# A two-layer attention and state-space trunk: states through the outputs' ring and one step ahead, last projections by token halves, zero products first, the last columns in parts

## The chip, the cores and the metric

The kernel runs on one core of a Trainium2 chip. The metric is the device time of one execution in microseconds (us), the median of several runs: less is better. TensorE is called PE, VectorE DVE or Vector, ScalarE ACT, GpSimd POOL; SyncE (SP) issues nearly all DMAs. Line numbers (L113) are those of the kernel before; in the changed kernel the same lines stand some two to thirty lines further down.

## The reference

A decoder trunk of two layers on 1024 tokens of width 1024, in float32. Each layer is x + RMSNorm(mixer(RMSNorm(x))).

```python
# layer 0: attention over three dilations (1, 4, 16), each a causal window of 129 keys, 16 heads of 64
proj = h @ w_in                       # queries, keys, values of 3 groups, and a gate z
o_g, lse_g = windowed_attention(q_g, k_g, v_g, rel_bias)
o = sum(softmax(lse)[g] * o_g)        # over the three groups
mixer = (o * silu(z)) @ w_out
# layer 1: a state-space layer, 64 groups of 16 channels, 64 complex states each
u, z = split(h @ w_in)
states = scan(a_bar, b_bar @ u)       # s[t] = a_bar * s[t-1] + bu[t]
y = Re(C @ states) + d * u
g = gelu(y)
y = g * sigmoid(g @ w_glu + b_glu)
mixer = (y * silu(z)) @ w_out
```

## The kernel before

Every large product is made of three matmuls: both operands are split into a rounded part and a rest (hi and lo: whi and wlo, hh and hl), and hi·hi, hi·lo and lo·hi are added in PSUM. One split is a cast on ACT and a subtraction on DVE or POOL (L86, L87). A projection of 128 output columns for 512 tokens (a token half, `th`) is 24 matmuls of 128x512 (`proj_half`). The order of instructions on every engine is fixed when the kernel is built, by a scheduler that follows the written order, the priorities (`high_priority`) and its own estimate of the times; each engine then works its list in order and waits where an input is missing.

**Start.** Eight tiles of 128 tokens are loaded. The gain of the norm, one row, is spread over all partitions by matmuls with a row of ones (tile `pg`, L747, copied by ACT at L748). Tile by tile (`norm_transpose0`) ACT sums the squares (L138), DVE finishes the norm (`rstd`, L73 to L78) and scales the tile by norm and gain in two halves (L143), PE transposes each half (`pst`, L130), ACT and DVE split it (hh, hl). The first values are projected at once (`psv`, L235 to L237) from weights `wvr`, which ACT casts and POOL subtracts.

**Layer 1.** The tiles of the attention's output are normed and transposed (`norm_transpose1`); the result is h1, four tiles of SBUF (hi and lo of two token halves) in the pool `pb`, whose slots are called b0 to b5. `in_order` then runs 16 projections, each for token half 0 and then 1, 32 steps of 24 matmuls (`psj`); the first eight give u, the last eight the gate z. The first two begin by halves of 256 columns, while the last tiles are still being transposed.

**The scan.** Between these steps stand the stages of eight channel groups e. Group e has its base at step t = (11e+2)/4 and each stage a distance d from it: loads, `ssm_input` (U, 5), `ssm_taps` (6), `ssm_states` (7), `ssm_outputs` (10). `ssm_states` multiplies BT and U (`pv`), turns and scans on DVE and POOL (T, L1381 to L1392) and leaves X (L1389 to L1393) in two tiles of half a group; `ssm_outputs` adds taps·U and CA·X (`py`, L1407 and L1408), puts the gelu together on ACT, POOL and DVE (Y) and stores it to DRAM (`y_dr`).

**GLU.** y is loaded again by token halves (`gy`, 16 loads of 128x512, L1476) into slots of a small ring and split into g0 and g1 (hi and lo, `pb`). The projections with w_glu start with a block: two weights, two token halves, products 0 to 6 of all four and then product 7 (`psb`, 96 matmuls). g0's lo part lies in b3, which the taps of groups 4 to 7 occupied; g1 lies in b4 and b5, which held h1's first half.

**Output.** `out_tiles` computes eight tiles of 128 tokens in two halves of 512 columns (`pso`); the last tile (`out_norm_last`) is normed at once and stored.

The pool `outs` (tag O, 4 buffers of 128x1024) serves the attention's outputs, z112 and the weights of the post norms (`post`).

Of the kernel before, what the change touches and what calls it, by code (L numbers as in the profile page):

```python
# [23 lines left out]
P = 128  # L24
# [9 lines left out]
EARLY = 4  # L34

# [679 lines left out]
def attention(c, a):  # L715
# [8 lines left out]
    with tc.tile_pool(name="vphase", bufs=1, side="right", reuse_waits="tile") as pool:  # L724
# [42 lines left out]
def in_order(c, srcs, h, use, after=None, start=None, ws=()):  # L767
# [109 lines left out]
def out_part(c, ps, g, w, i, n, ks):  # L877

    nc = c.nc
    gh, gl = g[i // 4]  # L880
    wh, wl = w[n]
    ts = slice(i % 4 * P, i % 4 * P + P)
    for n, k in ks:
        nc.tensor.matmul(ps, gh[:, k, ts], wh[:, k, :], start=n == 0, stop=False)  # L884
        nc.tensor.matmul(ps, gh[:, k, ts], wl[:, k, :], start=False, stop=False)  # L885
        nc.tensor.matmul(ps, gl[:, k, ts], wh[:, k, :], start=False, stop=n == KT - 1)  # L886
# [29 lines left out]
def out_norm_last(c, pss, post, x, done):  # L916

    nc = c.nc
    ss = c.small.tile([P, 2], F32, tag="ss2", name="ss2")
    ys = [c.slot("y") for _ in range(2)]  # L920
    sq = [c.slot("sq") for _ in range(2)]
    for n in range(2):
        nc.scalar.activation(sq[n], pss[n], AF.Square, accum_out=ss[:, n:n + 1])
        nc.vector.tensor_tensor(ys[n], pss[n], post[:, n * H:n * H + H], op=ALU.mult)
    r = rstd(c, ss)
    for n in range(2):
        ns = slice(n * H, n * H + H)
        nc.vector.scalar_tensor_tensor(x[:, ns], ys[n], r[:, 0:1], x[:, ns], op0=ALU.mult, op1=ALU.add)
        done(ns)


def out_tiles(c, g, w, post, res, done, order, late, last=None):
# [7 lines left out]
    for i in range(8):  # L940
# [4 lines left out]
        elif i < 7:  # L945
            for n in range(2):
# [3 lines left out]
        if i == 7 and last:  # L950
            out_norm_last(c, pss[i], post, x, lambda ns: last(x, ns))
# [416 lines left out]
def ssm_states(self):  # L1368
# [5 lines left out]
    self.X = []  # L1374
    for b in range(2):
        gs = slice(b * 4, b * 4 + 4)
        T1, T2, X = (c.ssm.tile([P, 4, P], F32, name=n, tag=n, bufs=2) for n in ("T1", "T2", "X"))
# [16 lines left out]
        self.X.append(X)  # L1394
# [28 lines left out]
def layer1(c, a, h1, ws):  # L1423
# [38 lines left out]
    for t in range(32, 39):  # L1462
        run(t)


def glu(c, a):
# [5 lines left out]
    for th, tags in enumerate((("b1", "b3"), ("b4", "b5"))):  # L1472
# [191 lines left out]
```

## Time and profile before

| | us |
|---|---|
| median of 3 runs (1678.32 to 1683.48) | 1678.59 |
| the profiled execution | 1679.3 |
| its span, first to last instruction | 1677.5 |
| PE busy | 1650.1 |
| DVE busy | 1011.9 |
| ACT busy | 712.2 |
| POOL busy | 460.0 |

The span is 1.8 us shorter than the profiled execution's time, and that execution is 0.7 above the median. A row of a timeline gives start, length, engine, line, operation, output and inputs, shape and count, and in brackets how long the engine was idle before it and what ended the idle time. A row of the waits gives engine, tile and line, what it waited for, the sum in us, how often, and the longest. A row of a group gives, after the bar, busy us and mean ns, then idle us before it and what ended most of it. A row of a stretch gives its length, then the busy us of PE, weight loads, DVE and ACT with their counts, the granted clock of PE, the DMA engines' share and GB/s.

### The profile page before, as it was taken

Reading aid. Unit: us, or ns where it says so; the run is one execution under the profiler, and the core shown is the slowest. Engines: PE = TensorE matmul, PEld = TensorE weight load, DVE = VectorE, ACT = ScalarE, POOL = GpSimd, SP = SyncE. Lnnn points to the kernel's source line nnn. Section 1 sums busy time; section 2 is a strip of 40 time slices with the busy share of each in tenths; the row PEclk is TensorE's granted clock in tenths of the full one; section 3 lists DMA queues with packets and bytes.
Section 4 is the critical chain, followed back from the end, with each engine's and each line's share of the span. In section 5 each row is a group of like instructions: output and inputs, shape, how many; then the busy total and the mean of one; then the engine's idle time right before and its main releaser. Section 6 shows DMA issues by size and latency. Waiting matters only on the chain.

```text
span 1677.5 us, 26337 instructions
## 1 busy us (share of the span) xinstructions
PE 1650.1 (98%) x9714; PEld 1390.6 (83%) x9714; DVE 1011.9 (60%) x2509; ACT 712.2 (42%) x1730; POOL 460.0 (27%) x303
## 2 busy tenths in 40 slices
PE   8999999999999999999999999999999999999998
PEld 6889999978888888888888888887788887867886
DVE  8698898625554554545455455557562888845533
ACT  5232223236455464645546464654452223343411
POOL 2000000131241514324161441404220344513121
PEclk9999999999999999999999999999999999989999
DMA  6213455531232414233252423318346979365432
GB/s 238 86 49 109 144 181 158 170 109 55 79 99 82 119 54 114 68 90 95 67 139 65 120 79 87 109 34 234 103 162 175 273 222 259 101 207 171 144 120 86
DMA packets 176857, 212.19 MB, mean 126 GB/s; under 512 B 37443, under 2 KB 133462, under 8 KB 176728
## 3 DMA queue, kind: packets, MB, share of 16 engines
q1 hardware_dynamic: 176728, 210.52, 42.3%
q8 instruction: 76, 1.25, 0.3%
q14 instruction: 53, 0.43, 0.1%
HBM read 153.51 MB, written 56.96 MB: 125 GB/s over the span
## 4 chain that ended last, share of the span: by engine, by line
PE 87%; DVE 7%; DMA 3%; issue 1%; POOL 1%; ACT 1%; SPq 0%; DVEq 0%; ACTq 0%; POOLq 0%
PE psj L113 46%; PE psq L376 11%; PE psl L474 5%; PE pso L551 4%; PE pt L502 4%; PE pso L886 3%; PE pso L885 3%; PE pso L884 3%; PE pso L577 1%; PE psb L113 1%; DVE T L1387 1%; PE psv L237 1%; DVE T L1392 1%; PE psv L236 1%; PE psv L235 1%
## 5 line engine op out<-in xcount | busy, mean ns | idle before, releaser
L113 PE MATMUL psj<-hh,wlo 128*128 128x512 f32 x896 | 358.2, 400 | 0.0
L113 PE MATMUL psj<-hh,whi 128*128 128x512 f32 x896 | 358.1, 400 | 0.0
L113 PE MATMUL psj<-hl,whi 128*128 128x512 f32 x896 | 355.2, 396 | 0.0
L87 POOL TENSOR_TENSOR wlo<-wraw,whi 128x1024 fp32r<-128x1024 f32 x48 | 115.2, 2399 | 395.9 <-ACT whi L86 380.8
L113 PEld LDWEIGHTS psj<-hh,whi 128*128 128x128 f32 x896 | 168.8, 188 | 37.0
L113 PEld LDWEIGHTS psj<-hh,wlo 128*128 128x128 f32 x896 | 168.8, 188 | 36.4
L113 PEld LDWEIGHTS psj<-hl,whi 128*128 128x128 f32 x896 | 168.7, 188 | 36.3
L491 ACT ACTIVATE lg<-lg,nm 128x128 f32<-128x128 f32 (+1 forms) x384 | 168.2, 442 | 37.3 <-DVE nm L486 37.3
L480 DVE CUSTOM_DVE_ANT_0 lg<-psl,T 128x128 f32<-128x128 f32 (+1 forms) x384 | 110.5, 347 | 88.7 <-PE psl L474 88.7
L86 ACT CAST whi<-wraw 128x1024 fp32r<-128x1024 f32 x80 | 83.7, 1046 | 163.8 <-PE psj L113 117.5
L376 PE MATMUL psq<-whi,v 128*128 128x256 f32 x640 | 120.3, 284 | 0.0
L87 DVE TENSOR_TENSOR ph<-pt,ph 128x512 fp32r<-128x512 f32 (+2 forms) x160 | 96.7, 622 | 15.3 <-ACT ph L86 13.1
L113 PE MATMUL psj<-h1h,whi 128*128 128x512 f32 (+1 forms) x272 | 105.0, 387 | 0.9 <-ACT h1h L86 0.9
L87 DVE TENSOR_TENSOR kl<-psj,kh 128x512 fp32r<-128x512 f32 x48 | 33.2, 692 | 120.1 <-ACT kh L86 119.5
L113 PE MATMUL psj<-h1l,whi 128*128 128x512 f32 (+1 forms) x272 | 104.1, 383 | 0.2 <-DVE h1l L87 0.2
L113 PE MATMUL psj<-h1h,wlo 128*128 128x512 f32 (+1 forms) x272 | 104.1, 383 | 0.0
L86 ACT CAST ph<-pt 128x512 fp32r<-128x512 f32 (+2 forms) x160 | 81.6, 530 | 46.5 <-PE pt L502 45.5
L376 PEld LDWEIGHTS psq<-whi,v 128*128 128x128 f32 x640 | 100.0, 189 | 1.2 <-issue 1.2
L376 PE MATMUL psq<-wlo,v 128*128 128x256 f32 x320 | 91.2, 286 | 0.7 <-DVE wlo L87 0.7
L551 PE MATMUL pso<-ph,vs 128*128 128x256 f32 (+1 forms) x544 | 86.6, 284 | 0.0
L502 PE MATMUL pt<-identr,lg 128*128 128x128 f32 x560 | 82.2, 276 | 0.0
L1253 POOL TENSOR_TENSOR Ks<-Ks,O 128x16 f32<-128x16 f32 x8 | 3.7, 462 | 284.0 <-ACT Ks L1251 284.0
(284 smaller groups left out, 3688.6 us busy)
## 6 DMA issues: line engine op xcount, KB each, us to landing
wraw<-in_w_in_dram SPq DMA_DIRECT2D x56, 512.0 KB
mw<-wt_dr SPq DMA_DIRECT2D x48, 256.0 KB
v<-in_w_v_dram SPq DMA_DIRECT2D x20, 512.0 KB
vp<-v_dr SPq DMA_DIRECT2D x16, 512.0 KB
wraw<-in_ssm_w_in_dram SPq DMA_DIRECT2D x16, 512.0 KB
v_dr<-v SPq DMA_DIRECT2D x30, 256.0 KB
rot_dr<-rt SPq DMA_DIRECT2D x48, 128.0 KB
ca_dr<-ca SPq DMA_DIRECT2D x32, 144.0 KB
```

The costliest lines, as they stand in the source:

```text
L86: c.last_hi = nc.scalar.copy(hi, src).ins
L87: return (engine or nc.vector).tensor_tensor(lo, src, f32(hi), op=ALU.subtract)
L113: nc.tensor.matmul(ps, a[:, s], b[:, k, :], start=first and k == 0 and n == 0, stop=k == KT - 1 and n == 2, skip_group_check=True)
L376: nc.tensor.matmul(o, r[x][:, k, ts], w[y][:, k, :], skip_group_check=True, start=i in (0, 4, 5) and t % 2 == k == n == 0, stop=k == 3 and ...
L474: nc.tensor.matmul(psl[:, h, o], x[HEADS[h], qs], y[HEADS[h], ks], start=j == js[0] and n == 0, stop=n == 2, skip_group_check=True)
L480: nc.vector.tensor_tensor_reduce(lg[:, h, j, 0:w], psl[:, h, o], bt[:, h, 256 - w:256], scale=1.0, scalar=-3.0e38, op0=ALU.add, op1=ALU.ma ...
L491: nc.scalar.activation(lg[:, h, j, 0:w], lg[:, h, j, 0:w], AF.Exp, bias=nm[:, h, b:b + 1], accum_out=ms[:, col:col + 1])
L502: c.nc.tensor.transpose(pt[:, n * P:(n + 1) * P], lg[:, h, j, part * P:part * P + P], c.ident)
L551: nc.tensor.matmul(o, l, r, start=n == 0, stop=n == len(jobs) - 1, skip_group_check=True)
L884: nc.tensor.matmul(ps, gh[:, k, ts], wh[:, k, :], start=n == 0, stop=False)
L885: nc.tensor.matmul(ps, gh[:, k, ts], wl[:, k, :], start=False, stop=False)
L886: nc.tensor.matmul(ps, gl[:, k, ts], wh[:, k, :], start=False, stop=n == KT - 1)
```

## The change

- **Zero products.** Eight matmuls of zeros (128x512, `idle`) stand first on PE; DVE writes the zeros first.
- **X in the ring O.** X of one group is one tile of the pool `outs`, with both halves, so that up to four groups can be alive. `ssm_input` stands at distance 4 and `ssm_states` at 6 for all groups but the first.
- **Last two projections by halves.** z's last two outputs (e = 14 and 15) are computed for token half 0 of both, then for half 1 of both.
- **GLU's inputs.** `gy` goes through three tiles of ring O, six half tiles, and may be issued only after the load of the last group's U. g0 lies in b1 and b4, g1 in b5 and b3.
- **Last columns in parts.** The second half of tile 7 is computed in two parts of 256 columns, each with its square and product by the post norm.

```diff
+IDLE = 8
@@ attention
+        zeros, idle = c.slot("zeros", F32R, tag="a"), c.psl.tile([P, H], F32, tag="psl", name="idle")
+        nc.vector.memset(f32(zeros), 0.0)
+        for n in range(IDLE):
+            nc.tensor.matmul(idle, zeros[:, 0:P], zeros, start=True, stop=True)
         nc.vector.memset(ones, 1.0)
@@ in_order
-    c.wide = 1 if start == "half" else c.wide
-    for e in range(len(ws), len(srcs)):
+    c.wide = int(start == "half")
+    pairs = 2 if start == "half" else 0
+    for e in range(len(ws), len(srcs) - pairs):
         w = load_w(c, srcs[e])
         for th in range(2):
             one(e, th, proj_half(c, w, h[th]))
+    ws = [(e, load_w(c, srcs[e])) for e in range(len(srcs) - pairs, len(srcs))]
+    for th in range(2):
+        for e, w in ws:
+            one(e, th, proj_half(c, w, h[th]))
@@ out_norm_last
+    ss = c.small.tile([P, 4], F32, tag="ss3", name="ss3")
+    ys = []
+    for n, (ps, cols) in enumerate(parts):
+        w = cols.stop - cols.start
+        y, sq = c.slot("y")[:, 0:w], c.slot("sq")[:, 0:w]
+        nc.scalar.activation(sq, ps, AF.Square, accum_out=ss[:, n:n + 1])
+        nc.vector.tensor_tensor(y, ps, post[:, cols], op=ALU.mult)
+        ys.append(y)
+        if n == 1:
+            nc.vector.tensor_tensor(ss[:, 3:4], ss[:, 0:1], ss[:, 1:2], op=ALU.add)
+    r = rstd(c, ss[:, 2:4])
+    for y, (ps, cols) in zip(ys, parts):
+        nc.vector.scalar_tensor_tensor(x[:, cols], y, r[:, 0:1], x[:, cols], op0=ALU.mult, op1=ALU.add)
@@ out_tiles
+            parts = [(pss[i][0], slice(0, H))]
+            for n in range(2):
+                cols = slice(n * 256, n * 256 + 256)
+                ps = c.psl.tile([P, H], F32, tag="psl", name="pso")[:, 0:256]
+                out_part(c, ps, g, w, i, 1, ks, cols)
+                parts.append((ps, slice(H + cols.start, H + cols.stop)))
@@ ssm_states
-        T1, T2, X = (c.ssm.tile([P, 4, P], F32, name=n, tag=n, bufs=2) for n in ("T1", "T2", "X"))
+    X2 = c.outs.tile([P, D], F32, tag="O", name="X", bufs=4).rearrange("p (b g n) -> p b g n", b=2, g=4)
+    self.X = [X2[:, b] for b in range(2)]
@@ layer1
-        for stage, d in ((ssm_loads, (-1, 2)[e] if e < 2 else 3), (ssm_input, 5), (ssm_taps, 6), (ssm_states, 7), (ssm_outputs, 10)):
+        for stage, d in ((ssm_loads, (-1, 2)[e] if e < 2 else 3), (ssm_input, 4 + (e == 0)), (ssm_taps, 6),
+                         (ssm_states, 6 + (e == 0)), (ssm_outputs, 10)):
@@ glu
-    for th, tags in enumerate((("b1", "b3"), ("b4", "b5"))):
+    ring = [x[:, n * H:n * H + H] for x in (c.outs.tile([P, D], F32, tag="O", name="gy", bufs=4) for _ in range(3)) for n in range(2)]
+    for th, tags in enumerate((("b1", "b4"), ("b5", "b3"))):
         for et in range(8):
-            y = c.slot("gy")
-            nc.sync.dma_start(y.rearrange("p (i n) -> p i n", i=4), y_view(c, et, th))
+            y = ring[(8 * th + et) % 6]
+            with tc.issue_after(last_input):
+                nc.sync.dma_start(y.rearrange("p (i n) -> p i n", i=4), y_view(c, et, th))
```

ACT's first instructions, before (ACTIVATE at L138 is a tile's sum of squares, `wvr` are the first value weights, `pg` the gain):

```order
L138 ACTIVATE v_117,ss<-v_118 128x1024
L748 COPY v_117<-pg 128x512
L86 CAST v_140<-wvr 128x1024 x2
L748 COPY v_117<-pg 128x512
L138 ACTIVATE v_117,ss<-v_118 128x1024
```

and of the change:

```order
L140 ACTIVATE v_117,ss<-v_118 128x1024
L88 CAST v_151<-wvr 128x1024
L755 COPY v_117<-pg 128x512
L88 CAST v_151<-wvr 128x1024
L140 ACTIVATE v_117,ss<-v_118 128x1024
L755 COPY v_117<-pg 128x512
```

The first cast of value weights has moved ahead of the first copy of the gain, and tile 1's sum of squares ahead of the second.

SP's list around the end of the scan, before (z_dr are stores of the gate, y_dr stores of y, gy the GLU's inputs; the two pairs of y_dr stores are those of groups 6 and 7):

```order
L1415 DMA y_dr<-Y_14745 128x512
L1415 DMA y_dr<-Y_14763 128x512
L1439 DMA z_dr<-z_14812 128x512
L98 DMA wraw<-in_w_glu_dram 128x1024
L1439 DMA z_dr<-z_14841 128x512
L1415 DMA y_dr<-Y_14845 128x512
L1415 DMA y_dr<-Y_14863 128x512
L1476 DMA gy<-y_dr 128x4x128 x3
L1439 DMA z_dr<-z_14912 128x512
L1476 DMA gy<-y_dr 128x4x128 x6
```

and of the change, from the first gy loads to the stores of group 7:

```order
L1506 DMA gy<-y_dr 128x4x128 x4
L1465 DMA z_dr<-z_14715 128x512
...
L1506 DMA gy<-y_dr 128x4x128 x2
L1441 DMA y_dr<-Y_14748 128x512
L1441 DMA y_dr<-Y_14766 128x512
L1465 DMA z_dr<-z_14821 128x512
L1506 DMA gy<-y_dr 128x4x128 x4
L984 DMA post<-in_ssm_post_norm_dram 128x1024
L1506 DMA gy<-y_dr 128x4x128
...
L1506 DMA gy<-y_dr 128x4x128 x2
L1441 DMA y_dr<-Y_14854 128x512
```

All gy loads stood behind the stores of group 7; now six stand ahead of those of group 6, and the load of the post norm's weights has come among them.

PE's last transposes for layer 1, before (`xn` is the normed tile):

```order
L113 MATMUL psj<-h1l_12779,whi 128x256
L130 MATMUL pst<-identr,xn 128x128 x4
L113 MATMUL psj<-h1h_12778,wlo 128x256
L130 MATMUL pst<-identr,xn 128x128 x4
L113 MATMUL psj<-h1h_12778,whi 128x256 x2
```

and of the change:

```order
L115 MATMUL psj<-h1l_12790,whi 128x256
L132 MATMUL pst<-identr,xn 128x128 x4
L115 MATMUL psj<-h1h_12789,wlo 128x256
L132 MATMUL pst<-identr,xn 128x128 x4
L115 MATMUL psj<-h1h_12789,whi 128x256
L115 MATMUL psj<-h1l_12790,whi 128x256
```

In the row "x2" the second of the two is the first product of the next 256 columns, which needs the tile just transposed; in the change nine more products of the first columns stand between. On PE the products pv and py of a group have 24 matmuls more between them for every group but the first. The last projections read, before: group 7's pv, 24 matmuls, group 6's py, 48, group 7's py, 48, psb; of the change: group 7's pv, 48, group 6's py, 48, group 7's py, 48, psb.

More of the change, by code (lines that the diff above doesn't have):

```diff
@@ L874, in attn_gate, with out_part @@
     return g, raw
-def out_part(c, ps, g, w, i, n, ks):
+def out_part(c, ps, g, w, i, n, ks, cols=slice(0, H)):
     nc = c.nc
@@ L883, in out_part @@
     for n, k in ks:
-        nc.tensor.matmul(ps, gh[:, k, ts], wh[:, k, :], start=n == 0, stop=False)
-        nc.tensor.matmul(ps, gh[:, k, ts], wl[:, k, :], start=False, stop=False)
-        nc.tensor.matmul(ps, gl[:, k, ts], wh[:, k, :], start=False, stop=n == KT - 1)
+        nc.tensor.matmul(ps, gh[:, k, ts], wh[:, k, cols], start=n == 0, stop=False)
+        nc.tensor.matmul(ps, gh[:, k, ts], wl[:, k, cols], start=False, stop=False)
+        nc.tensor.matmul(ps, gl[:, k, ts], wh[:, k, cols], start=False, stop=n == KT - 1)
 def out_bank(c, i):
@@ L913, in out_norm, with out_norm_last @@
         nc.gpsimd.tensor_tensor(x[:, ns], x[:, ns], y, op=ALU.add)
-def out_norm_last(c, pss, post, x, done):
+def out_norm_last(c, parts, post, x, done):
     nc = c.nc
-    ss = c.small.tile([P, 2], F32, tag="ss2", name="ss2")
-    ys = [c.slot("y") for _ in range(2)]
-    sq = [c.slot("sq") for _ in range(2)]
-    for n in range(2):
[L923 to L929, printed above, removed]
+    ss = c.small.tile([P, 4], F32, tag="ss3", name="ss3")
[11 more added lines that the diff above has]
+        nc.vector.scalar_tensor_tensor(x[:, cols], y, r[:, 0:1], x[:, cols], op0=ALU.mult, op1=ALU.add)
+    for n in range(2):
+        done(slice(n * H, n * H + H))
 def out_tiles(c, g, w, post, res, done, order, late, last=None):
@@ L945, in out_tiles @@
         elif i < 7:
-            for n in range(2):
+            for n in range(2 if i < 6 or not last else 1):
                 pss[i + 1][n] = out_half(c, g, w, i + 1, n, ks)
@@ L950, in out_tiles @@
         if i == 7 and last:
-            out_norm_last(c, pss[i], post, x, lambda ns: last(x, ns))
+            parts = [(pss[i][0], slice(0, H))]
[4 more added lines that the diff above has]
+                parts.append((ps, slice(H + cols.start, H + cols.stop)))
+            out_norm_last(c, parts, post, x, lambda ns: last(x, ns))
         else:
@@ L1373, in ssm_states @@
     lo, hi = slice(0, 64), slice(64, 128)
-    self.X = []
+    X2 = c.outs.tile([P, D], F32, tag="O", name="X", bufs=4).rearrange("p (b g n) -> p b g n", b=2, g=4)
+    self.X = [X2[:, b] for b in range(2)]
     for b in range(2):
         gs = slice(b * 4, b * 4 + 4)
-        T1, T2, X = (c.ssm.tile([P, 4, P], F32, name=n, tag=n, bufs=2) for n in ("T1", "T2", "X"))
+        T1, T2 = (c.ssm.tile([P, 4, P], F32, name=n, tag=n, bufs=2) for n in ("T1", "T2"))
+        X = self.X[b]
         pv = c.psl.tile([P, 4, P], F32, tag="psl", name="pv")
@@ L1393, in ssm_states @@
         nc.vector.tensor_tensor(X[:, :, 1:P], X[:, :, 1:P], T2[:, :, 0:P - 1], op=ALU.subtract)
-        self.X.append(X)
 def ssm_outputs(self):
@@ L1463, in layer1, with glu @@
         run(t)
-def glu(c, a):
+    return groups[7].load_U.ins
+def glu(c, a, last_input):
     nc, tc = c.nc, c.tc
@@ L1557, in trunk @@
         c.es_pa.close()
-        layer1(c, a, h1, ws)
+        last_input = layer1(c, a, h1, ws)
         c.es_pa.close()
         c.pa2 = c.es_pa.enter_context(tc.tile_pool(name="pa2", bufs=1, side="left", reuse_waits="tile"))
-        y2 = glu(c, a)
+        y2 = glu(c, a, last_input)
         w = [[c.pa2.tile([P, KT, H], F32R, tag=f"w0{x}", name=f"wf0{x}") for x in "hl"],
```

## The prediction

> **What bounds the kernel now.** I read the busy times, then the chain that ended last, then the waits of TensorE (PE) over the whole span.
>
> ```profile
> PE 1650.1 (98%) x9714; PEld 1390.6 (83%) x9714; DVE 1011.9 (60%) x2509; ACT 712.2 (42%) x1730; POOL 460.0 (27%) x303
> PE 87%; DVE 7%; DMA 3%; issue 1%; POOL 1%; ACT 1%; SPq 0%; DVEq 0%; ACTq 0%; POOLq 0%
> ```
>
> PE is busy for 1650.1 of 1677.5 us. Only 27.4 us can be won by waiting less, beside matmuls that run slower than they could. The waits by name show where those microseconds are:
>
> ```profile
> PE pg L747 <- DMA grow<-in_attn_pre_norm_dram: 4.3, 1, 4.3
> PE py L1408 <- DVE X L1393: 2.4, 1, 2.4
> PE pst L130 <- DVE vv L73: 1.7, 1, 1.7
> PE psb L113 <- ACT g1b L86: 1.4, 1, 1.4
> ...
> PE pso L886 <- DVE gl L87: 1.2, 1, 1.2
> PE py L1408 <- POOL Y L1412: 1.1, 1, 1.1
> PE pst L130 <- DVE hl L87: 1.0, 1, 1.0
> PE psj L113 <- ACT h1h L86: 0.9, 1, 0.9
> PE pso L884 <- ACT gh L86: 0.8, 1, 0.8
> ```
>
> Four places carry them: the start (pg, pst), the first tiles of layer 1 (psj), the scan (py), the start of the GLU (psb). The change touches all four, and the last tile. The pso waits are in the attention's output, which it does not edit.
>
> **The GLU's start.** All inputs of the block psb are now loaded and split around the end of the last projection.
>
> ```profile
> 1480.14 0.39 PE L113 MATMUL psj<-h1l,whi 128*128 128x512 f32 x1
> 1480.37 0.40 PE L113 MATMUL psj<-h1h,wlo 128*128 128x512 f32 x1
> 1487.58 1.22 PE L113 MATMUL psb<-g1b,whi 128*128 128x512 f32 x2 [1.44 <-ACT g1b L86]
> 1512.68 0.73 PE L113 MATMUL psj<-g0b,whi 128*128 128x512 f32 x2 [0.20 <-ACT whi L86]
> ```
>
> The first two rows give the pace of full 128x512 matmuls, 0.23 us from start to start. I use 0.234, the mean over this stretch's steady part. The last psj ends at about 1480.6, the next stage starts at 1512.68: 32.1 us for 96 matmuls, which at 0.234 need 22.5. So 9.6 us are lost. Where, the granted clock tells:
>
> ```profile
> 1480.60:1512.70 32.10, 27.58 (x96) 19.94 (x96) 0.00 (x0) 1.54 (x3) 0.84 0.72 215
> 1488.00:1492.00 4.00, 3.43 (x8) 2.22 (x8) 3.01 (x5) 2.27 (x4) 0.00 (x0) 0.50 1.10 350
> ```
>
> 4.5 us are idle (32.10 less 27.58 busy), the other 5.1 us come of the clock, 0.50 in the second row's stretch. Both go if the inputs stand ready, since then PE does not idle.
>
> ```profile
> 1476.73 1.58 SPq L1476 DMA_DIRECT2D gy<-y_dr  x3
> 1487.79 0.62 ACT L86 CAST g1b<-gy 128x512 fp32r<-128x512 f32 x1 [0.27 <-DMA gy<-y_dr]
> 1488.70 0.62 ACT L86 CAST g0b<-gy 128x512 fp32r<-128x512 f32 x1 [0.29 <-DMA gy<-y_dr]
> ```
>
> SP issues the first loads at 1476.73, after all outputs, and in the end a split follows every 0.9 us (the last two rows). In the changed order the first six of the sixteen gy loads (the ring's six half tiles) stand before group 6's output stores, and ten before the load of the post norm's weights. Their splits can be written early, because layer 1's h1 for the first token half is dead 48 matmuls (11.2 us) before psb. In 11.2 us twelve splits at 0.9 are done; the other four come under psb's own first products. The loads of group 7 are last, but their products stand last in the block too: from row 85 on, 84 x 0.234 = 19.7 us in. The load of the post norm's weights now waits on SP for group 7's X; six gy loads lie behind it, 5.4 us at that rate, less than the 11.2 us of matmuls left there. I take −9.0 of −9.6; the poor bound is half, −4.8, if SP's queue or Vector still lags.
>
> **The scan.** The states' X is a tile of a four-buffer ring instead of two halves, and the states stand one step earlier in the order.
>
> ```profile
> 1403.59 0.49 PE L1408 MATMUL py<-X,CA 128*128 128x128 f32 x2 [2.44 <-DVE X L1393]
> L1381 DVE TENSOR_TENSOR T<-Cg,pv 128x512 f32<-128x512 f32 x16 | 11.0, 688 | 24.7 <-PE pv L1380 24.4
> L1390 POOL MEMSET X<- 128x4 f32 x15 | 1.6, 104 | 30.6 <-PE py L1408 30.6
> ```
>
> PE needs X one subtraction too soon. From pv to py the changed order has 24 more matmuls, 24 x 0.234 = 5.6 us, against waits of 2.44 and 1.1 (the row py from POOL Y above). Vector sits idle for 24.7 us before it gets a new pv, so the lead can be used, and POOL's memset need no longer wait 30.6 us for py. Both waits go: −3.5, with 0 as the poor bound. Two X tiles and one U are live longer; they are there already, so no instruction is added.
>
> **The first tiles of layer 1.** The last tile's transposes move up.
>
> ```profile
> 1262.36 0.28 PE L113 MATMUL psj<-h1l,whi 128*128 128x256 f32 x1
> 1262.47 0.28 PE L113 MATMUL psj<-h1h,wlo 128*128 128x256 f32 x1
> 1264.27 1.34 ACT L159 ACTIVATE xn<-xr,rs_y 128x512 f32<-128x512 f32 x2 [1.25 <-DVE rs_y L78]
> 1267.82 0.60 PE L130 MATMUL pst<-identr,xn 128*128 128x128 f32 x4
> 1269.92 0.50 PE L113 MATMUL psj<-h1h,whi 128*128 128x256 f32 x2 [0.94 <-ACT h1h L86]
> ```
>
> xn ends near 1265.6, yet the transposes come at 1267.82. Nine 128x256 matmuls (0.12 us each, first two rows) now stand behind them: they come 1.07 us sooner and still after xn. The wait is 0.94, with a little behind it: −1.0 (0 to −1.1).
>
> **The last tile.** 48 matmuls of 256 columns (5.76 us at 0.12) replace 24 of 512 (5.62): +0.1. What follows the last one is smaller:
>
> ```profile
> 1669.47 0.60 ACT L923 ACTIVATE sq<-pso 128x512 f32<-128x512 f32 x1 [4.97 <-PE pso L886]
> 1670.26 0.69 DVE L924 TENSOR_TENSOR y<-pso,post 128x512 f32<-128x512 f32 x1 [4.97 <-ACT sq L923]
> ```
>
> Half of the width takes about 0.25 off each, a third final product on Vector (two of 256 columns for one of 512) and its small sum cost 0.1 or 0.2. Together −0.2 (−0.6 to +0.2).
>
> **The start.** Eight zero products run while the loads arrive. That is no gain by itself; what it could do is bring the real ones to full pace.
>
> ```profile
> 8.33 1.11 PE L130 MATMUL pst<-identr,v 128*128 128x128 f32 x4 [0.33 <-DVE v L143]
> 11.87 0.77 PE L235 MATMUL psv<-v,hh 128*128 128x512 f32 x1
> ...
> 15.43 0.63 PE L237 MATMUL psv<-v,hl 128*128 128x512 f32 x1
> 15.86 0.63 PE L235 MATMUL psv<-v,hh 128*128 128x512 f32 x1
> 19.76 0.66 PE L130 MATMUL pst<-identr,v 128*128 128x128 f32 x4 [0.96 <-DVE hl L87]
> ```
>
> The psv products from 11.87 to 15.86, nine steps, take 0.43 each and another like them, instead of 0.234: 2 us. But PE waits again at 19.76, so part of a quicker head turns into a longer wait. And the same edit moves ACT: the cast of the first value weights now stands ahead of the copy of the gain.
>
> ```profile
> 6.33 0.59 ACT L748 COPY v<-pg 128x512 f32<-128x512 f32 x1 [0.81 <-PE pg L747]
> 6.91 1.04 ACT L86 CAST v<-wvr 128x1024 fp32r<-128x1024 f32 x1
> 7.52 0.75 DVE L143 SCALAR_TENSOR_TENSOR v<-v,rs_y,v 128x512 f32<-128x512 f32 x1
> 8.03 5.26 POOL L87 TENSOR_TENSOR v<-wvr,v 128x1024 fp32r<-128x1024 f32 x2 [7.59 <-ACT v L86]
> 9.76 1.30 DVE L143 SCALAR_TENSOR_TENSOR v<-v,rs_y,v 128x512 f32<-128x512 f32 x1 [1.48 <-ACT v L748]
> ```
>
> Today the first half of tile 0 is scaled (7.52) before POOL starts at 8.03; the second is scaled while POOL works, and takes 1.30 instead of 0.75, to 11.06. POOL's two operations end near 10.66 and 13.29: the long one ends with the first. If POOL now starts first, near 7.9, both scalings run into it: the first ends near 10.5 instead of 8.3, the second with POOL's next, near 13.2 instead of 11.06. That is some +2.1 for the transposes. Against it stand the 2 us of pace, part of which the wait at 19.76 takes back (up to 1 us). The splits of later tiles also stand behind more scaling rows on Vector, and the value weights' second pair puts POOL to work once more: up to one more POOL operation, 2.6 (half of 5.26). I take +2.5, a little above the first lock alone, between −2 (pace won, no lock) and +4.7 (2.1 and 2.6).
>
> The Trainium skill, SBUF — State Buffer, section SBUF: two separate sides, says that POOL and a Vector operation with two tensors in SBUF exclude each other for a whole instruction; the long 1.30 row agrees, and by this rule the scaling indeed waits to POOL's end. The Trainium skill, TensorE: Matmul & The Clock Gate, section Part 1: The HAM clock gate, states that some 3.4 us of busy window bring full pace; by this rule alone the start would gain the 2 us. Here PE works from 8.33 at the latest, and is slow still at 15.86, so the trace agrees in direction, not in the time it takes.
>
> **The sum.** −9.0 − 3.5 − 1.0 − 0.2 + 2.5 = −11.2 on the profiled execution's 1679.3 us: 1668.1. That execution is 0.7 above the median 1678.59, so about 1667.4 against the median; I say 1668. The pso waits (2.0 together) stay, with ±1 for the rows around them that moved.
>
> **Rivals.** About 5 us, 0.3%, is what a measurement can tell from no change.
>
> 1. Forecast as above, 1664 to 1672: 0.57.
> 2. *The GLU's wait moves.* SP holds the gy loads behind the post weights' wait, or Vector's splits lag. For it: SP is in order, and 6 of 16 loads lie behind. Against it: 11.2 us of matmuls cover them. Half the gain, so 1668 + 4.2 = 1672; with the scan's waits kept as well, 1675.5. 0.17, of which 0.08 ends within 0.3%.
> 3. *The start gains.* Full pace from the first transposes, POOL not in the way: 1668 − 4.5 = 1663.5. For it: the 0.42 steps; against it: ACT's new row. 0.14.
> 4. *The change does not do what it says:* the waits of scan and GLU stay, the first tiles and the tail win 1.2, the start loses 2.5: 1680. For it: both stages depend on rows that other engines issue in order. 0.06, nearly all of it within 0.3%.
> 5. *Slower: Vector's order in the scan.* The states of group e+1 now stand ahead of the weights' splits (wlo) and outputs of group e. Where POOL lengthens Vector's rows (as at L143: 1.30 for 0.75), a projection waits for wlo. It decides once a step's Vector work passes the time of its matmuls; the 24.7 us idle over 8 groups (3 each) is the margin, and speaks against it. A wait of 1.2 us (one such lengthened pair of rows) in each of 14 projections costs 16.8: 1668 + 16.8 = 1685. 0.06.
>
> The range is 1662 to 1677: rival 3 below, most of rival 2 above, and it leaves out rivals 4 and 5 and some of the low side. Faster by over 0.3% (below 1673.6): forecast 0.57, rival 3 0.14, and 0.09 of rival 2: 0.80. Within 0.3%: 0.08 of rival 2 and 0.06: 0.14. Slower: 0.06.
>
> **What would show it.** Right: no psb wait over 0.3 us and a granted clock of 1.00 from the last projection on, with the 96 products in about 22.5 us; no py wait; the psj wait at the first tiles near 0.1; the first transposes later than 8.33, with L143's two rows over 1 us each beside POOL. Wrong: psb waits that name gy or g1b again; projections in the scan that wait for wlo; unbroken matmuls from before 19 us on, which is rival 3; a new long wait in the attention's output. The prediction falls if the time is above 1673.6.

## The result, and the profile after

The changed kernel takes 1668.29 us (median of five, 1666.20 to 1670.63) against 1678.59 for the kernel before in the same runs: a measured ratio of 0.9921, interval 0.9907 to 0.9934. It is not the ratio of these two medians, which is 0.9939: the five runs of the kernel before spread over 5.5 us (1677.96 to 1683.48), so the size of the gain, 0.6 to 0.9%, is known less well than its sign. The profiled execution took 1668.29 with a span of 1666.5 us, 11.0 less than the 1677.5 before. That is the predicted number, but it is not the predicted sum: several terms came out otherwise, and the largest single term of all stood in no part of the working.

The profile's page of the changed kernel, busy times and chain of waits:

```profile
PE 1640.4 (98%) x9746; PEld 1389.8 (83%) x9746; DVE 1020.5 (61%) x2513; ACT 709.6 (43%) x1732; POOL 469.7 (28%) x303
PE 88%; DVE 6%; DMA 3%; issue 1%; POOL 1%; ACT 1%; SPq 0%; DVEq 0%; ACTq 0%; POOLq 0%
```

PE has 32 more instructions than before and is nevertheless busy for 9.7 us less (1640.4 against 1650.1). So most of the gain is not waiting at all: matmuls became shorter. The waits of PE by name (total, times, longest, in us) say the same from the other side:

```profile
PE psj L115 <- DVE wlo L89: 4.6, 1, 4.6
PE pst L132 <- DVE vv L75: 4.0, 1, 4.0
PE pst L132 <- DVE hl L89: 2.2, 2, 1.8
PE psb L115 <- ACT whi L88: 1.8, 1, 1.8
PE psq L378 <- DVE wlo L89: 1.5, 2, 1.2
PE idle L746 <- DVE zeros L744: 1.5, 1, 1.5
```

Before, the list was led by the load of the gain (4.3), py (2.4) and pst (1.7). The py waits are gone and the psb waits are down to one, but two waits of over 4 us have come that were not there: a projection in the scan for the low part of its weights (wlo), and the first transposes for a normed tile.

To set the stages side by side, I cut both traces at the first matmul of each stage. "Idle" is PE without work, "half pace" what steps of 512-column matmuls over 0.36 us take beyond 0.234, and "pace" is all the rest, in us, before and after. A wait ahead of a stage's first matmul counts with the stage before it. The time ahead of PE's very first matmul (4.25 us before, 1.45 after) stands in the start's pace. The psq products are the products of layer 0 that are computed by quarters, from the weights and hh, hl or a tile v; they have 256 columns, and pv and py have 128, so a half clock behind one of their waits stands in their pace.

| Stage | whole | idle | half pace | pace | difference |
|---|---|---|---|---|---|
| start (to layer 0's first psj) | 66.58, 72.16 | 3.19, 7.12 | 5.05, 7.41 | 58.34, 57.63 | +5.6 |
| first gates (psj) | 44.62, 44.64 | 0, 0 | 0, 0 | 44.62, 44.64 | 0 |
| psq products | 219.23, 216.16 | 0.66, 1.87 | 0, 0 | 218.57, 214.29 | −3.1 |
| attention | 822.33, 821.68 | 0, 0 | 1.00, 0.96 | 821.33, 820.72 | −0.7 |
| its output | 97.38, 95.10 | 2.01, 0.88 | 0.32, 0.32 | 95.05, 93.90 | −2.3 |
| layer 1 and scan | 231.21, 230.00 | 5.23, 6.64 | 0.17, 1.64 | 225.81, 221.72 | −1.2 |
| GLU's block psb | 31.33, 24.19 | 3.71, 0.34 | 4.98, 1.91 | 22.64, 21.94 | −7.1 |
| rest of the GLU | 68.22, 66.63 | 0, 0 | 0.77, 0.69 | 67.45, 65.94 | −1.6 |
| output | 88.07, 87.93 | 0, 0 | 0, 0 | 88.07, 87.93 | −0.1 |

The tail behind the last matmul brings the remaining −0.5. Behind the start the pace column falls by 12.5 in all, more than the whole gain, and the largest part of it in the psq products, which the change does not edit. Each kernel has one trace, and the waits of a stage can differ from one kernel to the next where no edit touched it: those of the psq products are 0.7 to 5.3 us over all the kernels below.

**The start**, from the timeline of the changed kernel (start, duration, engine, line, instruction; in brackets the idle time before it and what ended it):

```profile
5.16 2.10 PE L754 MATMUL pg<-grow,ones 1*128 1x512 f32 x4
...
7.20 1.04 ACT L88 CAST v<-wvr 128x1024 fp32r<-128x1024 f32 x1 [1.70 <-DMA wvr<-in_w_v_dram]
8.15 0.58 ACT L755 COPY v<-pg 128x512 f32<-128x512 f32 x1
8.32 5.13 POOL L89 TENSOR_TENSOR v<-wvr,v 128x1024 fp32r<-128x1024 f32 x2 [7.88 <-ACT v L88]
8.76 2.47 DVE L145 SCALAR_TENSOR_TENSOR v<-v,rs_y,v 128x512 f32<-128x512 f32 x1 [0.80 <-ACT v L755]
11.29 1.12 PE L132 MATMUL pst<-identr,v 128*128 128x128 f32 x4 [4.03 <-DVE vv L75]
11.59 2.40 DVE L145 SCALAR_TENSOR_TENSOR v<-v,rs_y,v 128x512 f32<-128x512 f32 x1
13.08 0.79 PE L237 MATMUL psv<-v,hh 128*128 128x512 f32 x1 [0.68 <-ACT hh L88]
13.67 0.63 PE L238 MATMUL psv<-v,hh 128*128 128x512 f32 x1
...
31.84 0.65 PE L132 MATMUL pst<-identr,v 128*128 128x128 f32 x4 [1.85 <-DVE hl L89]
```

POOL starts at 8.32, before the first scaling at 8.76, and both scalings run 2.4 us instead of 0.75 and 1.30. PE stands for 4.03 us, and the value products start at half pace (13.08 to 13.67). The clock by windows (stretch, its length, busy times of the engines, and then the granted clock):

```profile
12.00:16.00 4.00, 3.33 (x11) 2.25 (x11) 4.00 (x15) 3.53 (x7) 1.45 (x1) 0.50 1.02 415
34.00:36.00 2.00, 2.00 (x6) 1.51 (x6) 2.00 (x8) 1.07 (x2) 0.00 (x0) 0.50 0.02 6
1456.60:1458.60 2.00, 1.96 (x5) 1.57 (x6) 1.67 (x2) 0.00 (x0) 1.12 (x1) 0.50 0.40 70
```

Three times a wait is followed by a half clock: the 4.03 at the first transposes, the 1.85 at 31.84, and the scan's 4.56 in the next timeline. The kernel before waited 2.44 us for X at 1403.59, and its granted clock stayed at 1.00 (1403.5 to 1415), so the length of the one wait does not decide it alone.

**The end of the scan and the GLU's start**, from the same timeline:

```profile
1448.68 1.05 ACT L88 CAST whi<-wraw 128x1024 fp32r<-128x1024 f32 x1
1448.71 1.36 DVE L1414 TENSOR_TENSOR_SCAN T<-rho,T 128x128 f32<-128x128 f32 x4
...
1452.37 1.00 DVE L1419 TENSOR_TENSOR T<-Sg,T 64x512 f32<-64x512 f32 x1
1453.47 1.56 DVE L1420 TENSOR_TENSOR X<-X,T 128x508 f32<-128x508 f32 x1
1454.96 1.62 DVE L89 TENSOR_TENSOR wlo<-wraw,whi 128x1024 fp32r<-128x1024 f32 x1
1456.64 0.80 PE L115 MATMUL psj<-h1h,wlo 128*128 128x512 f32 x1 [4.56 <-DVE wlo L89]
...
1478.13 0.62 ACT L88 CAST g1b<-gy 128x512 fp32r<-128x512 f32 x1 [2.64 <-DMA gy<-y_dr]
1478.65 1.04 ACT L88 CAST whi<-wraw 128x1024 fp32r<-128x1024 f32 x1
1479.74 1.03 PE L115 MATMUL psb<-g0b,whi 128*128 128x512 f32 x2 [1.85 <-ACT whi L88]
```

Vector computes the states of the last group (the rows of L1414 to L1420) ahead of the low part of the last projection's weights, and PE waits for it. Behind, the first weights of the GLU stand on ACT behind a cast that waits for its gy load.

### The profile page after: what moved, and what is told of

The parts are those of the page before. It is cut to its first block, busy times and chain, and to the rows that moved or that the text cites. A ratio compares the mean times of both kernels' runs of the same rounds, so it can differ in the third digit from the quotient of the medians.

```text
span 1666.5 us, 26394 instructions
## 1 busy us (share of the span) xinstructions
PE 1640.4 (98%) x9746; PEld 1389.8 (83%) x9746; DVE 1020.5 (61%) x2513; ACT 709.6 (43%) x1732; POOL 469.7 (28%) x303
## 4 chain that ended last, share of the span: by engine, by line
PE 88%; DVE 6%; DMA 3%; issue 1%; POOL 1%; ACT 1%; SPq 0%; DVEq 0%; ACTq 0%; POOLq 0%
PE psj L115 47%; PE psq L378 10%; PE psl L476 5%; PE pso L553 4%; PE pt L504 4%; PE pso L897 3%; PE pso L899 3%; PE pso L898 3%; PE pso L579 1%; PE psb L115 1%; PE psv L239 1%; PE psv L238 1%; DVE wlo L89 1%; PE psv L237 1%; DVE T L1414 1%
## 5 line engine op out<-in xcount | busy, mean ns | idle before, releaser
L378 PE MATMUL psq<-whi,v 128*128 128x256 f32 x640 | 115.6, 280 | 0.0
```

The costliest lines, as they stand in the source:

```text
L378: nc.tensor.matmul(o, r[x][:, k, ts], w[y][:, k, :], skip_group_check=True, start=i in (0, 4, 5) and t % 2 == k == n == 0, stop=k == 3 and ...
```

## The experiments

None of the twelve kernels leaves out a part of the computation: unused bytes, zero products, buffers or an order differ. The kernel before took 1678.6 us on the first chip and 1682.6 to 1683.2 on those of the batches below, so times of different batches are compared by their ratio to the kernel before of the same batch.

**Where the pace came from.** The new tile `ss3` has three slots of 32 bytes each in the pool of small scalars. In the built program most tiles allocated behind that pool on the same side (the projection weights whi and wlo, the ring, layer 0's hh) lie 96 bytes further in each partition; those allocated from the other side (layer 1's h1h and h1l, the GLU's inputs, the values) stay. The first batch puts the same bytes into the kernel before, unused, and takes them out of the changed one.

```diff
 e1_pad96, on the kernel before (e2_pad32 with [P, 8], e3_pad64 with [P, 16])
         c.small = pool("small", bufs=3)
+        c.small.tile([P, 24], F32, tag="pad", name="pad", bufs=1)
```

```diff
 e4_changed_noshift, on the changed kernel
-    ss = c.small.tile([P, 4], F32, tag="ss3", name="ss3")
+    ss = c.small.tile([P, 4], F32, tag="ss2", name="ss3")
```

> The kernel before with one unused tile of 96 bytes per partition behind the small scalars, and nothing else: every instruction in the same order, but the weights (whi, wlo), the ring and the left pools start 96 bytes later, as they do in the changed kernel, while the tiles of the right side (h1h, h1l, g0b, v) stay. Theory A, the pace of a matmul depends on where its two operands lie relative to one another: the pace of layer 1 falls from 0.234 to 0.229 and the time from 1678.6 to about 1667 (the stretches of PE that are neither idle nor at half clock were 12.5 shorter in the changed kernel). Theory B, the pace came with the changed order or with the run: 1678.6, pace 0.234.

> The same with 32 bytes. Theory A with a period of 64 bytes (h1h at 131040 and whi at 15680 differ by 32 modulo 64, and by 96 bytes more by 0): as quick as with 96 bytes, about 1667. Theory A with a longer period: somewhere between 1667 and 1679. Theory B: 1678.6.

> The same with 64 bytes. Theory A with a period of 64 bytes: as slow as before, 1678.6. Theory A with a longer period: anything from 1667 to 1679, and other than with 32. Theory B: 1678.6.

> The changed kernel with the last tile's four sums in the slots of the earlier two sums, so that nothing is moved by 96 bytes; the order of all instructions is that of the changed kernel. Theory A: the pace falls back to 0.234 in layer 1, and the time goes from 1668.3 to about 1680, that is, all the rest of the change together wins nothing. Theory B: 1668.3, pace 0.229.

| Kernel | us | ratio to before | interval |
|---|---|---|---|
| before + 96 bytes | 1672.84 | 0.9950 | 0.9931 to 0.9969 |
| before + 32 bytes | 1677.91 | 0.9967 | 0.9954 to 0.9980 |
| before + 64 bytes | 1681.19 | 0.9997 | 0.9987 to 1.0007 |
| change, tiles in their old places | 1676.68 | 0.9966 | 0.9956 to 0.9977 |

96 unused bytes, with every instruction in its old order, make the kernel before 0.5% faster. One stretch of layer 1's projections shows how. The kernel before (two products of the same kind, 18 steps apart):

```profile
1431.29 0.40 PE L113 MATMUL psj<-h1l,whi 128*128 128x512 f32 x1
...
1435.50 0.40 PE L113 MATMUL psj<-h1l,whi 128*128 128x512 f32 x1
```

the same kernel with the 96 bytes, again 18 steps apart:

```profile
1427.39 0.40 PE L113 MATMUL psj<-h1l,whi 128*128 128x512 f32 x1
...
1431.52 0.39 PE L113 MATMUL psj<-h1l,whi 128*128 128x512 f32 x1
```

4.21 against 4.13 us for 18 steps: 0.2339 and 0.2294 each; the changed kernel has 0.2294 as well. Nothing waits there. The groups of PE between 1280 and 1470 us (busy, then the mean ns of one) show the gain in the means too; with them the psq products with v, between 120 and 320 us. Before:

```profile
L113 PE MATMUL psj<-h1l,whi 128*128 128x512 f32 x204 | 80.8, 396 | 0.0
L376 PE MATMUL psq<-whi,v 128*128 128x256 f32 x608 | 114.0, 284 | 0.0
```

with the 96 bytes:

```profile
L113 PE MATMUL psj<-h1l,whi 128*128 128x512 f32 x203 | 78.9, 389 | 0.0
L1407 PE MATMUL py<-U,taps 128*128 128x128 f32 x128 | 26.4, 290 | 0.0
L376 PE MATMUL psq<-whi,v 128*128 128x256 f32 x608 | 109.4, 280 | 0.0
```

changed:

```profile
L115 PE MATMUL psj<-h1l,whi 128*128 128x512 f32 x205 | 80.2, 391 | 0.0
```

and changed, with the tiles in their old places:

```profile
L115 PE MATMUL psj<-h1l,whi 128*128 128x512 f32 x208 | 82.4, 396 | 0.0
```

Which products gain fits the placement. Those with one operand moved and one not do: psj of layer 1, and psq with v, whose median step falls from 0.120 to 0.114 us with the bytes and in the change, and is 0.120 again with the tiles in their old places. Those whose two operands both moved keep their step: psq with hh has 0.119 in all four, and the 192 products of the first gates (hh and whi) take 44.6 to 44.8 us. Not every product with one operand moved gains: py of U and taps has a median step of 0.112 us in all.

The mean of 290 ns of py in the padded kernel, against 275 in the kernel before and in the changed one, is no matter of placement. In one of the eight groups PE waits 2.88 us for X, and the clock behind is at half:

```profile
1397.17 0.80 PE L1408 MATMUL py<-X,CA 128*128 128x128 f32 x2 [2.88 <-DVE X L1393]
1397.00:1400.00 3.00, 2.83 (x13) 2.83 (x14) 3.00 (x5) 0.00 (x0) 0.00 (x0) 0.50 0.89 242
```

The half clock costs about 2.9 us there: the 32 products of the group take 9.60 us, the wait included, against 6.27 in the kernel before, whose wait is 2.44. By stages the padded kernel's pace falls by 4.6 us in the psq products, 1.2 in attention's output, 0.7 in layer 1 (3.6 without that half clock) and 1.5 in the rest of the GLU, where the changed kernel has 4.3, 1.2, 4.1 and 1.5. With the tiles in their old places the gain of pace is gone: 219.2 us in the psq products and 225.2 in layer 1, against 218.6 and 225.8 in the kernel before, and within 0.3 of it in the other stages behind the start. Without the move the change keeps 0.34%, 5.7 us, where about 1680 and no gain at all had been expected; the product of the two ratios, 0.9950 x 0.9966 = 0.9916, meets the 0.9921 of both together. The 64 bytes win nothing by the whole time (0.9997, interval up to 1.0007), so more distance is not simply better. The 32 bytes cannot be told from the 96 by the whole time, but the traces differ: the pace of the psq products is 217.9 us with 32 and 214.1 with 96, so the period of 64 bytes that had been considered does not hold.

**Is it the distance of the two operands?** The ring was moved a second time, in the changed kernel without its zero products (the next experiment, which is the basis here).

```diff
 e9_no_zeros_ring64 (e10_no_zeros_ring32 with [P, 8])
         c.ring = pool("ring", bufs=1)
+        c.ring.tile([P, 16], F32, tag="pad", name="pad")
         c.outs = pool("outs", bufs=1)
```

> The changed kernel without zero products and with an unused tile of 64 bytes ahead of the ring: the weights whi and wlo stay where they are in the changed kernel, while the ring, the outputs' ring and the left pools with hh, hl, woh, wf0, U and X start 64 bytes later. Theory A (the pace is one of the distance between a matmul's two operands): the projections of layer 1, whose h1h and whi both stay, keep their pace (h1l,whi 0.226, h1h,wlo 0.229), while those of layer 0 (hh and whi), which had one pace of 0.2325 in all kernels so far, change; if a distance of 64 modulo 128 is quick there as it is for h1, they fall to 0.228 and the time by up to 2688 x 0.0045 = 12 us against the same kernel without the 64 bytes (ratio to the kernel before near 0.982 instead of 0.989). Rival, the place of the weights alone sets the pace: nothing changes in layer 0, ratio 0.989.

> The same with 32 bytes ahead of the ring: the distance of hh and whi becomes 32 modulo 64, which is that of h1h and whi in the kernel before (0.234). Theory A: layer 0's projections slow to about 0.234, 2688 x 0.0015 = 4 us more, ratio near 0.9915; attn_out (woh and gh) goes to the slow distance too, +1.5. Rival, the place of the weights alone: ratio 0.989 and 0.2325.

With 64 bytes: 1665.91 us, 0.9905 (0.9878 to 0.9931). With 32: 1672.08, 0.9938 (0.9918 to 0.9958). Against the basis the pace of attention, where PE never idles, rises by 1.9 and 4.1 us, while that of the psq products falls by 2.0 and rises by 1.9 (the latter with 1.2 more of waits than the basis, so half clock may be in it). Layer 1 keeps its pace to 0.4, as it should, since neither h1 nor the weights moved. So the placement of a tile that no edit names moves whole stages by microseconds, in both directions; but the speed-up of layer 0's projections that the first of the two was to bring did not come. The 192 products of the first gates take 44.63 us in the basis, 44.80 with 64 bytes and 44.98 with 32: the rival, that the place of the weights alone counts, is out, since the weights did not move. The slow-down that had been expected of the 32 bytes, 4 us in layer 0 and 1.5 in attention's output, did come (4.1 in attention, 1.4 in its output), though the whole time rose by more than expected (0.9938, where 0.9915 was worked out). What function of the two places sets the step stays open.

**The zero products.**

```diff
 e5_changed_no_zeros
-        zeros, idle = c.slot("zeros", F32R, tag="a"), c.psl.tile([P, H], F32, tag="psl", name="idle")
-        nc.vector.memset(f32(zeros), 0.0)
-        for n in range(IDLE):
-            nc.tensor.matmul(idle, zeros[:, 0:P], zeros, start=True, stop=True)
```

```diff
 e6_changed_4_zeros
-IDLE = 8
+IDLE = 4
```

```diff
 e11_changed_8_zeros_copy_first: the casts of the value weights may be issued only after the first copy of the gain
-        split(c, wh[k // 4][:, k % 4:k % 4 + 2], wl[k // 4][:, k % 4:k % 4 + 2], raw,
-              engine=nc.gpsimd)
+        with c.tc.issue_after(c.gain0):
+            split(c, wh[k // 4][:, k % 4:k % 4 + 2], wl[k // 4][:, k % 4:k % 4 + 2], raw,
+                  engine=nc.gpsimd)
```

> The changed kernel without the zero products and their tile; ACT's order at the start is then that of the kernel before (copy of the gain, then the casts). Theory: the start of the changed kernel lost 5.6 (first psj at 72.2 instead of 66.6), because the cast that stands ahead starts POOL before the first scaling, and Vector's scaling waits for POOL. Without the zeros the first psj comes near 66.6 again, and the time falls from 1668.3 to about 1663. Rival: the zero products themselves or the pace carry the start, and the first psj stays near 72; 1668.

> The changed kernel with four zero products instead of eight; with four the scheduler keeps ACT's order of the kernel before, so that the products stay and the order goes. If the order is what cost the start: first psj near 66.6 and about 1663, as without zeros. If full pace can be had early by zero products: near 64.6, about 1661. If the zero products as such cost the start: near 70.

> The changed kernel with its eight zero products, but the value weights' casts held behind the first copy of the gain on ACT. If ACT's order is what makes POOL win the race against the first scaling: the scaling (128x512, line L145 or near) starts before POOL and takes 0.75, the first transposes come near 8.6 instead of 11.3; first psj near 67 or, if full pace holds from the zero products, near 65; time about 1663 to 1664. If POOL still starts first by a hair: transposes near 10.8, first psj near 69, 1666.

| Kernel | us | ratio to before | interval | start stage |
|---|---|---|---|---|
| changed, no zero products | 1664.58 | 0.9891 | 0.9873 to 0.9909 | 66.89 |
| changed, 4 zero products | 1665.52 | 0.9895 | 0.9875 to 0.9915 | 68.62 |
| changed, copy of the gain first | 1665.66 | 0.9899 | 0.9877 to 0.9920 | 68.29 |

Without zero products (timeline):

```profile
7.82 0.75 DVE L145 SCALAR_TENSOR_TENSOR v<-v,rs_y,v 128x512 f32<-128x512 f32 x1
8.06 5.52 POOL L89 TENSOR_TENSOR v<-wvr,v 128x1024 fp32r<-128x1024 f32 x2 [7.62 <-ACT v L88]
8.62 1.11 PE L132 MATMUL pst<-identr,v 128*128 128x128 f32 x4 [0.66 <-DVE v L145]
```

with four:

```profile
7.88 5.11 POOL L89 TENSOR_TENSOR v<-wvr,v 128x1024 fp32r<-128x1024 f32 x2 [7.45 <-ACT v L88]
7.90 5.64 DVE L145 SCALAR_TENSOR_TENSOR v<-v,rs_y,v 128x512 f32<-128x512 f32 x2
```

and with eight, the copy first:

```profile
5.17 3.78 PE L755 MATMUL pg<-grow,ones 1*128 1x512 f32 x4
7.89 0.75 DVE L145 SCALAR_TENSOR_TENSOR v<-v,rs_y,v 128x512 f32<-128x512 f32 x1 [0.18 <-ACT v L756]
8.88 4.69 POOL L89 TENSOR_TENSOR v<-wvr,v 128x1024 fp32r<-128x1024 f32 x2 [8.44 <-ACT v L88]
11.31 2.81 DVE L145 SCALAR_TENSOR_TENSOR v<-v,rs_y,v 128x512 f32<-128x512 f32 x1
11.82 0.80 PE L238 MATMUL psv<-v,hh 128*128 128x512 f32 x1 [1.83 <-ACT hh L88]
```

Which of two engines starts first decides it: a scaling at 7.82, 0.24 ahead of POOL, takes 0.75; one at 7.90, 0.02 behind POOL, is stuck (two take 5.64). With ACT's order put right by hand, the first scaling is free again, but the second still meets POOL. Nor did the zero products bring the real ones to full pace: the gain's products pg take 3.78 us after eight of them in this trace, though 2.10 in the changed kernel's own, and the value products begin with long steps in each trace, with zero products or without. In all six traces with zero products PE waits for 1.8 us or more between them and the value products. Without them the start takes 66.89, about the 66.58 of the kernel before, and the whole kernel has the lowest ratio of all here: 0.9891. It beats the kernel before by 1.1% and the changed one's 0.9921 with an interval that just overlaps (0.9909 and 0.9907 at the near ends). Its start is 5.3 us shorter than the changed kernel's, but attention's output takes 2.5 us of that back (97.59 against 95.10). Four of them, or eight with the copy first, lie between in the start, and cannot be told apart from none by the whole time.

**The states one step ahead, and the GLU's inputs.**

```diff
 e7_changed_old_distances
-        for stage, d in ((ssm_loads, (-1, 2)[e] if e < 2 else 3), (ssm_input, 4 + (e == 0)), (ssm_taps, 6),
-                         (ssm_states, 6 + (e == 0)), (ssm_outputs, 10)):
+        for stage, d in ((ssm_loads, (-1, 2)[e] if e < 2 else 3), (ssm_input, 5), (ssm_taps, 6),
+                         (ssm_states, 7), (ssm_outputs, 10)):
```

```diff
 e8_changed_old_glu_inputs
-    pairs = 2 if start == "half" else 0
+    pairs = 0
...
-    for th, tags in enumerate((("b1", "b4"), ("b5", "b3"))):
+    for th, tags in enumerate((("b1", "b3"), ("b4", "b5"))):
...
-            y = ring[(8 * th + et) % 6]
-            with tc.issue_after(last_input):
-                nc.sync.dma_start(y.rearrange("p (i n) -> p i n", i=4), y_view(c, et, th))
+            y = c.slot("gy")
+            nc.sync.dma_start(y.rearrange("p (i n) -> p i n", i=4), y_view(c, et, th))
```

> The changed kernel with the distances of U and the states back at 5 and 7; X stays in the ring, the last pairs and the GLU's inputs stay as changed. Theory: the states one step ahead removed 3.5 of py waits and brought 4.6 of a psj wait for wlo with 1.5 of half clock behind it, so undoing it moves the time from 1668.3 to about 1666 (py waits again, no wlo wait). Rival, the lead is the gain in the scan: 1671 or more.

> The changed kernel with the last pairs in the old order and the GLU's inputs through the small ring into the old tiles. Theory: the early inputs took the block psb from 31.3 to 24.2 us and its wait ahead from 0.6 to 1.9, so undoing them brings psb waits for gy and half clock back: from 1668.3 to about 1674. Rival, the block's gain is one of pace only: 1669.

The old distances: 1670.82 us, 0.9925 (0.9903 to 0.9947). Its waits of PE:

```profile
PE py L1434 <- DVE X L1420: 3.3, 1, 3.3
PE psj L115 <- DVE wlo L89: 2.5, 1, 2.5
PE psb L115 <- ACT whi L88: 0.7, 1, 0.7
```

The py wait is back, and the wait for wlo is down from 4.6 to 2.5, that for the GLU's first weights from 1.85 to 0.7 (one of 0.9 for g1b has come in psb). In layer 1 PE idles for 6.73 us in all, with the states ahead for 6.64. So the earlier states remove their wait and hand it on to the next rows of Vector and ACT. Layer 1 takes 2.1 us longer here (232.10 against 230.00), about 2 of it half clock among the py products behind the 3.3 us wait. Undoing the lead had been expected to win 2 us; by the ratios, 0.9925 and the changed kernel's 0.9921, nothing is won, and the two cannot be told apart.

The old GLU inputs: 1673.02 us, 0.9938 (0.9918 to 0.9959). Its waits of PE:

```profile
PE psb L115 <- ACT g1b L88: 2.3, 1, 2.3
PE psb L115 <- ACT g0b L88: 2.1, 2, 1.8
```

Here neither py nor a psj waits for more than 0.3 us: the scan runs free with the states ahead. Layer 1 takes 223.79, 6.2 less than in the changed kernel, and the block psb 30.13, 5.9 more. In these two stages the early inputs and the halves together have won nothing (253.9 against 254.2 us). By the ratios this kernel is 2.9 us slower than the changed one (their intervals overlap), where 5.7 had been expected: the psb waits and their half clock did come back, but layer 1 won as much. The run undoes the halves and the early inputs together, so it does not say which of them brings the wait for wlo. As for the rest, what the old inputs' profile loses elsewhere is 0.6 us in the start and 4.6 in the psq products, where its waits for wlo are 3.9 us instead of 1.5.

**Can the wait for wlo be taken away?**

```diff
 e12_no_zeros_wlo_on_pool, on the changed kernel without zero products
-    ws = [(e, load_w(c, srcs[e])) for e in range(len(srcs) - pairs, len(srcs))]
+    for e in range(len(srcs) - pairs, len(srcs)):
+        c.w_engine = c.nc.gpsimd if e == len(srcs) - 1 else c.nc.vector
+        ws.append((e, load_w(c, srcs[e])))
...
-            split(c, g[th][0][:, et, :], g[th][1][:, et, :], y)
+            with tc.issue_after(last_hi):
+                split(c, g[th][0][:, et, :], g[th][1][:, et, :], y)
```

> The changed kernel without zero products; of the last projection's weights (e = 15) POOL makes the rest wlo instead of Vector, and the first GLU casts stand behind that weight's cast on ACT. Theory: the 4.2 to 4.6 wait of a psj for wlo comes of Vector's list, in which the states of group 7 stand ahead of wlo; on POOL wlo stands behind two products of X only (about 1451.8 plus 2.4 for the operation), so the wait shrinks to 2 or less, the half clock behind it goes, and the time falls by 2 to 4 against the same kernel without this (ratio to before near 0.987 instead of 0.989). Rival, wlo is late because its weights or its buffer are late: the wait stays above 4.

1665.60 us, 0.9901 (0.9884 to 0.9917), no better than its basis (0.9891, 0.9873 to 0.9909). PE's waits at the end of the scan:

```profile
1454.17 0.50 PE L115 MATMUL psj<-h1h,wlo 128*128 128x512 f32 x1 [2.21 <-POOL wlo L89]
1478.15 1.22 PE L115 MATMUL psb<-g0b,whi 128*128 128x512 f32 x2 [4.08 <-ACT whi L88]
```

The low part comes sooner from POOL, the wait falls from 4.2 to 2.2, and the half clock behind it is gone. But ACT's first casts for the GLU, held back for that, now make the GLU's first weights late by 4.08. So wlo was late mainly because of Vector's list, as expected, and not because of its weights or its buffer; but the expected 2 to 4 us did not come. ACT has the same work as before at this place, and the new order chose which product pays.

## Why the prediction came out right, and where it was wrong

**The total.** 1668 was predicted and 1668.29 measured, a meeting of errors that cancel: that the number fits is luck. The profiled sum was −11.2; the profile gave −11.0, from these terms:

| Step of the prediction | predicted | measured |
|---|---|---|
| GLU's start | −9.0 | −5.9 |
| scan | −3.5 | waits −3.5, and a new wait with its half clock +6 |
| first tiles | −1.0 | −0.9 |
| last tile | −0.2 | about −0.5, all of the tail |
| start | +2.5 | +5.6 |
| pso waits | 0 | −1.1 |
| waits of the psq products | 0 | +1.2 |
| pace of matmuls | not considered | −12.5, of which 0.7 is in the GLU's row |

**The pace** is the error that matters. The prediction took 0.234 us per full matmul for both kernels and counted only idle time and clock. The step that failed is a term put at nothing without a reason: the change of pace, −12.5 us. The tile `ss3` stood in its last tile's term only as a sum that costs 0.1 or 0.2; that it moves other tiles was not considered. Two runs show this cause from both sides, the bytes alone (0.9950) and the change without them (0.9966). Which products gained, those with one operand moved, says the same. By the latter run the change itself is worth 5.7 us, half of the predicted 11.2 and near 1673 on the first chip's scale: inside the range, but near the time of the prediction's second rival (1672).

**The GLU's start** was right in its mechanism: six gy loads ahead of the stores, the splits done early, the load of the post norm's weights no obstacle, and 96 products in 24.19 us without a wait for gy or g1b by PE. From the last projection to the next stage it is 32.1 us before and 26.2 after. The shortfall against 9.0 is the 1.85 us wait for whi and the 1.91 of half pace behind it, and it has rival 2's form: a cast that waits for its load stands on ACT ahead of something urgent. The prediction looked at SP's queue and Vector for that and did not follow ACT's list. The range of this term (−4.8 to −9.6) held it. The wait for whi is not in every kernel with the early inputs: without zero products, with four, and with the copy first no psb wait is over 0.3 us, and the block takes 22.5 to 23.6 us, near the 22.5 predicted; why was not followed up. But by the run with the old inputs the two edits for this place win nothing net: the 5.9 us that psb gains are paid in layer 1 (6.2).

**The scan** was right on the removed waits and wrong on what follows. The step that failed is "so the lead can be used": Vector's 24.7 us of idle time were counted over all the groups, while the lead is needed at one place, where group 7's states, the outputs of the earlier group and the last weights meet. Rival 5 named this mechanism, a projection that waits for wlo behind the states, and it did happen, but once (4.56 us and a half clock of about 1.5) instead of fourteen times. Two orders of the change meet there: the states ahead, and the last two projections by halves, which need e = 15's weights 24 matmuls sooner. With the halves and the old distances the wait is 2.5; with the states ahead, the GLU's old inputs and no halves it is not there. A projection that waits for wlo was one of the signs of being wrong that the prediction had named.

**The first tiles and the tail** came as worked out: 0.23 of the psj waits is left of 0.94 and 0.22 (the h1l row of the same tile), and the last square and product take 0.38 and 0.42 us instead of 0.60 and 0.69.

**The start** was right in sign and in its lock: POOL first, both scalings long, the first transposes at 11.29 (the first scaling was to end near 10.5; it ended at 11.23). The term was undersized by 3.1, outside its own bounds (−2 to +4.7), because the consequences were taken one at a time. Behind the 4.03 us of waiting the clock was at half, so the pace that the zero products were to bring was gone, a split that comes late made a second wait (1.85 at 31.84), and that one a second half clock. The upper bound added one POOL operation, but no clock. The Trainium skill, TensorE: Matmul & The Clock Gate, section Part 1: The HAM clock gate, states that the clock falls after an idle window of about 3.4 us. The 4.03 and 4.56 us waits agree with it, the half clocks after waits of 1.85 us (34 to 36 us) and, in the padded kernel, 2.88 do not, so here shorter waits cost clock too, if not every one: the 2.44 of the kernel before cost none.

**The pso waits** fell by 1.1; the prediction had left them at 0 with ±1. The traces tie this to the zero products: PE idles for 0.4 to 1.1 us in attention's output in the six kernels that have them and for 1.6 to 2.2 in the eight that have none. By which rows they do it was not followed.

## What to carry to other kernels

A change that adds a tile, however small, moves the tiles behind it, and a kernel bound by matmuls can gain or lose half a per cent by that alone: time the kernel before with the same bytes added, unused, before giving an edit the credit. Where a wait is removed, look at each engine's list at that one place, not at its idle time over the stage: the wait for X became one for wlo, and moved to POOL it became one for whi. Before warming up an engine, look at what waits behind it: here PE waited again after the zero products in every trace, and the instructions that came with them changed which of two engines started first.

## What the runs showed of the hardware that was not expected

- The step of unbroken matmuls depends on where their two operands lie relative to each other: 0.2339 or 0.2294 us for 128x512 and 0.120 or 0.114 for 128x256 with 96 bytes of difference. By the whole time 32 and 96 bytes win (0.9967 and 0.9950) and 64 do not (0.9997). The rule behind it was not found.
- Two engines that start 0.02 us apart can cost 2 us: 7.90 after 7.88 turned two scalings into 5.64 us, where the one ahead of POOL took 0.75.
- A wait of 1.85 or 2.88 us was followed by a granted clock of 0.50, one of 2.44 us by 1.00.
- Zero products do not reliably bring full pace: after eight of them, four equal products took 2.10 us in one kernel's trace and 3.78 in another's.
